# A hybrid decoder layer on one core: the order of requests, splits, evacuations and constants in the first stage is changed

## The chip, the core and the metric

The program runs on one NeuronCore of a Trainium2 chip, in one launch. TensorE multiplies, VectorE and ScalarE split and evacuate, GpSimd does side work and issues DMAs on a queue of its own, and SyncE issues the large loads. The metric is the device time of a run in microseconds. Three runs of the kernel before took 1409.1, 1410.75 and 1412.94 us, with a median of 1410.75. The trace is of a further, profiled execution.

## The reference

One layer over 1024 tokens of width 1024, in float32:

```python
h = rms_norm(x, norm_mix)
z = h @ w_in                       # u, v of a gated MLP; q, k, values of attention
u, v = gelu(zu), gelu(zv)          # spatial gating, 4 groups, chunks of 128 tokens
a_out = u * (tril(W_s) @ layer_norm(v) + b)
lam = exp(sum(lq1*lk1)) - exp(sum(lq2*lk2)) + lambda_init
o = diff_attention(q, k, vv, lam)  # 4 heads, 2 causal softmax maps each, ALiBi
o = rms_norm(o, diff_subln) * (1 - lambda_init)
x = x + concat(a_out, o) @ w_out
x = x + memory_attention(rms_norm(x, norm_xq), rms_norm(mem, norm_mem), w_q, w_kv, w_o)
x = x + hierarchical_moe(rms_norm(x, norm_ffn), ...)   # 4 groups of 8 experts, top 2
return rms_norm(x, norm_final)
```

`mem` has 256 tokens; its keys and values are `rms_norm(mem) @ w_kv`, 2048 columns in all.

## The kernel before

Matmuls that need float32 accuracy are made of three. Each operand is split into a rounded part and a rest: ScalarE writes the first (`whi`, `hTh`, `mh`), VectorE subtracts and writes the second (`wlo`, `hTl`, `ml`), and `mm3` adds three products. Lines 141 to 143 are these three matmuls; lines 285 and 286 split a weight tile, 150 and 151 a scaled activation.

All weights come as tiles of 128 x 1024 (512 KB) in the order of one list, `plan`. `pump` requests tiles on SyncE's queue up to `ahead["load"]` tiles beyond the one in use and splits up to `ahead["split"]` beyond it; `take` hands out the next one. SBUF is 45 slots of one tile (`unit`), which a request may have to wait for. Smaller things lie in 7 half slots (`half`): the copies of memory's keys and values (`km`), and the scaled q or k (`pr`). PSUM has four single banks (`ps1`) and two double ones (`ps2`). The copies that the kernel makes by DMA (`kmd`, `vmd`, the halves of k) go out on GpSimd's queue.

The work is in three parts, each a run of generators in `merge`, which advances a clock of its own by the costs and delays that they yield and so interleaves them. In the first part the engines' order is exactly the order in which the code is recorded. In the second and third a scheduler orders TensorE, VectorE and ScalarE by a timeline of its own, and what it finds ready early it places among the last instructions of the first part; SyncE and GpSimd keep the recorded order. Then the experts follow, again in recorded order. Because the scheduler works on, a change in the first part also moves instructions in the next.

The first part, where the change is:

- `x_prep` (line 428) loads x transposed, eight tiles of 128 x 1024, and for each k splits it to `hTh`, `hTl`. The square of tile k-1 (in place, line 434, after its split has read it) stands behind that; even squares are added up by VectorE, odd ones by GpSimd (line 436). Behind the eighth tile the sums meet (452), eight small matmuls and a reciprocal root give the norm `xcol`, and transposes spread it to `rx` (464, 466). The splits don't wait for the norm: it is multiplied in when a product is evacuated.
- `first_qk` (line 505) multiplies each x tile, as it comes, with the weights of q and k of head 0: 12 matmuls of 512 columns per tile, into the two double banks `pd`. When `rx` is there, `evacs` (line 553) evacuates them: multiply by `rx` (472), round (566 or 577), subtract (567 or 579); the halves of k are also copied to the other 64 partitions by DMA (578, 580), for q's and k's rounded and rest parts are stacked.
- `mem_kv` (line 314) makes memory's keys and values: 16 weight tiles, each 24 matmuls of 256 columns (`pmk`), copied (329) and stored (330). Before the first it loads and splits memory itself, two tiles (`memt`, `mh`, `ml`). In tiles 9 and 10 memory is squared and reduced (336, 337); the norm `mcol` follows at the end (343), and `mem_row` (345) transposes it to a row (354).
- The constants come when `rx` is done, in the order in which the generator is reached: `sgu_consts` (735; line 737 requests the SGU weights, 738 masks them on GpSimd), `sgu_bias` (746; a matmul of the masked weights with ones, 749, and four additions, 751), `attn_consts` (536, lambda), `small_consts` (1005).

The scores of the second part (`scores`, lines 632 and 633) multiply q tiles with `ka` and `la`, then `kb` and `lb`, into the same two double banks, and add a bias (635) that GpSimd makes (612, 614).

Of the kernel before, what the change touches and what calls it, by code (L numbers as in the profile page):

```python
# [13 lines left out]
OP = mybir.AluOpType  # L14
# [48 lines left out]
R2 = 0.009  # L63
AT = 2.6
LIM = "q2:sc0 v1:sc0 q3:sc1"
A0 = 1
A1 = 5
A2 = 3
A3 = 2
RC = ('P', 3, 1)  # L70
PS = 4
# [43 lines left out]
def tile_layer(tc, a, out):  # L115
# [12 lines left out]
    def unit(name, shape, dt=F32):  # L128
        return up.tile(shape, dt, name=name, tag="u", bufs=NU)
# [182 lines left out]
    mrow = {}  # L312

    def mem_kv(i):
        if i == 0:
            for q in range(2):
                load_mem(q)
                split_mem(q)
                yield 0.0, 0.0
        for c in range(4 * i, 4 * i + 4):  # L320
            wh, wl = take()
            p = ps1("pmk")
            for k in range(KT):
                q, r = divmod(k, 4)
                mm3(p[:, :256], wh[:, k], wl[:, k], mhl[q][0][:, r], mhl[q][1][:, r], k == 0, k == KT - 1)
                if k == 3:
                    yield 1.3, 0.0
            km = half("km", (128, 256))
            nc.scalar.copy(km, p[:, :256])
            nc.gpsimd.dma_start((kmd, vmd)[c // 8][:, c % 8, :], km)  # L330
            yield 1.3, 0.0
            if c in (9, 10):
                q = c - 9
                if q == 0:
                    macc[0] = half("macc", (128, 2, 256))
                nc.scalar.activation(memt[q], memt[q], AF.Square)
                red(macc[0][:, q], memt[q].rearrange("p k t -> p t k"), axis=AX.X, op=OP.add)
        if i < 3:
            return
        pm = ps1("pm")  # L340
        for t in range(2):
            for q in range(2):
                mm(pm[:, 2 * t:2 * t + 2], macc[0][:, q, t * 128:(t + 1) * 128], ones[:, 0:2], start=(q == 0),
                   stop=(q == 1))
        rsq(mcol, pm[:, 0:4:2], D, 1e-6, "m")
        done.add("mcol")
# [163 lines left out]
    def first_qk(hd):  # L510

        w = [take() for _ in range(2)]
        p = [ps2() for _ in range(2)]
        for k in range(KT):
            for x in until(("x", k)):
                yield x
            for i in range(2):
                for h in range(2):
                    hs = slice(h * H, (h + 1) * H)
                    mm3(p[i][:, hs], w[i][0][:, k], w[i][1][:, k], hTh[k][:, hs], hTl[k][:, hs], k == 0, k == KT - 1)  # L520
            yield 2.56, 0.0
        done.add("first")
        ahead["load"], ahead["split"] = A1, A2
        for x in until("rx"):
            yield x
        qk[hd] = []
        for evac, q in zip(evacs(hd), p):
            for h in range(2):
                evac(h, q[:, h * H:(h + 1) * H])
                yield 0.0, 0.0  # L530
        done.add(("qk", hd))


# [4 lines left out]
    def attn_consts():  # L538
        for i, n in enumerate(("lambda_q1", "lambda_k1", "lambda_q2", "lambda_k2")):
            row(lam4[:, i], a[n], 64)  # L540
        nc.gpsimd.dma_start(subg, a["diff_subln"])
        for i in range(2):
            nc.vector.scalar_tensor_tensor(lam4[:, 2 * i], lam4[:, 2 * i], 1.0, lam4[:, 2 * i + 1], op0=OP.mult,
                                           op1=OP.mult, accum_out=lam[:, i:i + 1])
        nc.scalar.activation(lam[:, 2:4], lam[:, 0:2], AF.Exp)
        nc.vector.scalar_tensor_tensor(lam[:, 0:1], lam[:, 2:3], 0.8 - 0.6 * math.exp(-0.0), lam[:, 3:4],
                                       op0=OP.add, op1=OP.subtract)

# [4 lines left out]
    def evacs(hd):  # L553


        r0, r1 = slice(0, 64), slice(64, 128)

        def evac_q(h, p):
            hs = slice(h * H, (h + 1) * H)
            if h == 0:  # L560
                qk[hd] += [unit(n, [128, S], F32R) for n in ("qa", "qb")]
            qa, qb = qk[hd]
            q = scaled(h, p)
            sc = 0.125 / slopes[hd]
            for t, r, o in ((qa, r0, r1), (qb, r1, r0)):
                nc.scalar.activation(t[r, hs], q[r], AF.Copy, scale=sc)
                nc.vector.scalar_tensor_tensor(t[o, hs], q[r], sc, t[r, hs].bitcast(F32), op0=OP.mult,
                                               op1=OP.subtract)

        def evac_k(h, p):  # L570
            hs = slice(h * H, (h + 1) * H)
            if h == 0:
                qk[hd] += [unit(n, [128, S], F32R) for n in ("ka", "kb", "la", "lb")]
            ka, kb, la, lb = qk[hd][2:]
            k = scaled(h, p)
            for t, l, r, o in ((ka, la, r0, r1), (kb, lb, r1, r0)):
                nc.scalar.copy(t[r, hs], k[r])
                KQ(nc).dma_start(t[o, hs], t[r, hs])
                nc.vector.tensor_sub(l[r, hs], k[r], t[r, hs].bitcast(F32))
                KQ(nc).dma_start(l[o, hs], l[r, hs])  # L580

        return evac_q, evac_k

    def proj_qk(hd):
        qk[hd] = []
        for evac in evacs(hd):
            for x in proj_t(evac):
                yield x
        done.add(("qk", hd))
# [20 lines left out]
    def scores():  # L610
# [5 lines left out]
        for hd in range(4):  # L616
            for x in until(("qk", hd)):
                yield x
            qa, qb, ka, kb, la, lb = qk.pop(hd)
            for i in range(8):  # L620
                if 8 * hd + i - 2 * ndone[0] >= NA:
                    yield 0.0, lambda: 8 * hd + i - 2 * ndone[0] < NA
# [112 lines left out]
    def sgu_consts():  # L735
        w = unit("sgw", [128, 2, 4, 128])
        nc.gpsimd.dma_start(w[:, 0], a["sgu_wT"].rearrange("g s t -> s g t"))
        nc.gpsimd.affine_select(w[:, 0], w[:, 0], pattern=[[0, 4], [1, 128]], compare_op=OP.is_ge, fill=0.0, base=0,
                                channel_multiplier=-1)
        lg = sm.tile([128, 8], F32, name="lngb")  # L740
        nc.gpsimd.dma_start(lg[:, 0:4], a["sgu_ln_g"])
        nc.gpsimd.dma_start(lg[:, 4:8], a["sgu_ln_b"])
        row(w[:, 1].rearrange("p g t -> p (g t)"), a["sgu_b"], 512)
        sg["w"], sg["g"] = w, lg

    def sgu_bias():
        w, lg = sg["w"], sg["g"]
# [576 lines left out]
    nc.sync.dma_start(gmix, a["norm_mix"])  # L1324
    ahead["load"], ahead["split"] = 1, 1
    pump()
    ahead["load"] = A0
    gm[0] = col("norm_mem")
    gxq = col("norm_xq")
    gffn = col("norm_ffn")  # L1330
# [2 lines left out]
    def side(text):  # L1333

        g = [sgu_gate(i) for i in range(2) if "s%d" % i in text]
        if "k3" in text:
            g.append(mem_row())
        return g

    merge.run(x_prep(), *side(SEQ1), run_items(SEQ1.split()[0]),  # L1340
              seq(until("first"), run_items(SEQ1[3:])), seq(until("rx"), now(sgu_consts), now(sgu_bias), now(attn_consts),
                                                            now(small_consts)))
    man.__exit__(None, None, None)
    ahead["load"], ahead["split"] = AL, A3
    man = tc.manual_schedule(engines=ORDS[1])
# [348 lines left out]
```

## Time and profile before

| | |
|---|---|
| median of three runs | 1410.75 us (1409.1 to 1412.94) |
| profiled execution | 1409.82 us, its span 1408.1 us |
| TensorE, VectorE, ScalarE, GpSimd busy | 94%, 71%, 59%, 19% of the span |
| first stage (to the last memory matmul) | about 0 to 94 us |
| bytes moved | 322.39 MB, 229 GB/s on average |

The profile is one execution. "PE" is TensorE, "DVE" VectorE, "ACT" ScalarE, "POOL" GpSimd, "SPq" SyncE's queue. In a timeline a row is: start, duration, engine, line, operation, out<-in, shapes, count, and in brackets the idle time of the engine before it and what ended it. [...] Matmuls overlap, so a matmul's row is longer than its share of the time. The duration of a row with a count above 1 is that of all of them together.

### The profile page before, as it was taken

The page shows a single profiled execution, that of the slowest core. Times are in us where ns is not written, and L with a number is a line of the kernel's source. Part 1 is how long each engine was busy: PE and PEld are TensorE (multiplying, and loading weights), DVE is VectorE, ACT ScalarE, POOL GpSimd, SP SyncE. Part 2 cuts the span into 40 slices and gives each one's busy share as a digit, 9 for nine tenths or more (in the row PEclk, how much of TensorE's full clock was granted, in tenths as well). Part 3 has the DMA queues.
Part 4 walks back from the last instruction along what each step waited for, and adds up shares of the span by engine and source line. Part 5 has one row for each costly group of instructions (what it writes and reads, how often), then busy time and mean ns, then how long its engine had stood idle before and what let it go on. Part 6 is the DMA issues. An engine that isn't in the chain of part 4 may idle for free. (4 is left out here: it accounts for less than half of the span.)

```text
span 1408.1 us, 20553 instructions
## 1 busy us (share of the span) xinstructions
PE 1325.6 (94%) x7424; PEld 1148.1 (82%) x7424; DVE 1001.1 (71%) x1594; ACT 833.9 (59%) x1138; POOL 262.0 (19%) x287
## 2 busy tenths in 40 slices
PE   7889999999989999999999799999999999999981
PEld 5889898889887888999888587888777888888861
DVE  6646785676856444333454798999979999999975
ACT  7534463455454453333232588888868888888863
POOL 3231110301102231112112111111111111111012
PEclk9989999999999999999999799999999999999996
DMA  8550211212265666012689899999999699999985
GB/s 307 156 139 2 61 46 60 76 39 61 76 220 198 210 216 210 1 61 81 224 319 324 275 327 377 367 358 358 354 373 331 224 369 381 371 356 363 375 288 225
DMA packets 103225, 322.39 MB, mean 229 GB/s; under 512 B 15747, under 2 KB 23971, under 8 KB 103120
## 3 DMA queue, kind: packets, MB, share of 16 engines
q1 hardware_dynamic: 76896, 272.14, 52.8%
q0 software_dynamic: 17776, 40.51, 10.3%
q10 hardware_dynamic: 8448, 8.39, 1.8%
q8 instruction: 59, 0.97, 0.3%
q14 instruction: 46, 0.38, 0.1%
HBM read 287.10 MB, written 46.66 MB: 237 GB/s over the span
## 5 line engine op out<-in xcount | busy, mean ns | idle before, releaser
L286 DVE TENSOR_TENSOR wlo<-raw,whi 128x1024 fp32r<-128x1024 f32 (+1 forms) x469 | 556.2, 1225 | 84.5 <-ACT whi L285 72.7
L285 ACT CAST whi<-raw 128x1024 fp32r<-128x1024 f32 (+1 forms) x469 | 471.6, 1049 | 62.9 <-DVE wlo L286 11.2
L141 PE MATMUL pgu<-whi,xth 128*128 128x512 f32 x512 | 198.7, 397 | 4.5 <-ACT whi L285 3.4
L142 PE MATMUL pgu<-wlo,xth 128*128 128x512 f32 x512 | 200.9, 392 | 1.1 <-DVE wlo L286 1.1
L143 PE MATMUL pgu<-whi,xtl 128*128 128x512 f32 x512 | 200.4, 391 | 0.5 <-DVE xtl L147 0.5
L1424 POOL DMA_INDIRECT x2d<-y,idx x31 | 50.3, 1621 | 450.0 <-ACT y L1423 412.4
L141 PEld LDWEIGHTS pgu<-whi,xth 128*128 128x128 f32 x512 | 96.8, 189 | 26.1 <-ACT whi L285 5.3
L142 PEld LDWEIGHTS pgu<-wlo,xth 128*128 128x128 f32 x512 | 96.8, 189 | 22.6 <-DVE wlo L286 2.5
L143 PEld LDWEIGHTS pgu<-whi,xtl 128*128 128x128 f32 x512 | 96.7, 189 | 21.1 <-DVE xtl L147 1.2
L141 PE MATMUL py<-whi,ht 128*128 128x512 f32 x256 | 103.0, 402 | 4.4 <-ACT whi L285 2.2
L142 PE MATMUL py<-wlo,ht 128*128 128x512 f32 x256 | 104.4, 408 | 2.2 <-DVE wlo L286 2.1
L143 PE MATMUL py<-whi,ht 128*128 128x512 f32 x256 | 101.1, 395 | 0.0
L639 ACT ACTIVATE p<-p,stt 128x128 f32<-128x128 f32 (+7 forms) x64 | 49.6, 776 | 49.7 <-DVE stt L638 40.8
L142 PE MATMUL pp<-wlo,hTh 128*128 128x256 f32 x256 | 73.1, 285 | 1.5 <-DVE wlo L286 1.5
L141 PE MATMUL pp<-whi,hTh 128*128 128x256 f32 x256 | 73.4, 287 | 0.2 <-ACT whi L285 0.2
L141 PE MATMUL pp<-whi,h2h 128*128 128x256 f32 x256 | 73.1, 285 | 0.0
L143 PE MATMUL pp<-whi,hTl 128*128 128x256 f32 x256 | 72.8, 285 | 0.0
L142 PE MATMUL pp<-wlo,h2h 128*128 128x256 f32 x256 | 72.5, 283 | 0.0
L143 PE MATMUL pp<-whi,h2l 128*128 128x256 f32 x256 | 72.5, 283 | 0.0
L141 PE MATMUL pp<-hTh,whi 128*128 128x512 f32 x160 | 64.3, 402 | 0.4 <-ACT ot L691 0.4
L142 PE MATMUL pp<-hTl,whi 128*128 128x512 f32 x160 | 63.6, 398 | 0.0
L143 PE MATMUL pp<-hTh,wlo 128*128 128x512 f32 x160 | 63.5, 397 | 0.0
(365 smaller groups left out, 2956.9 us busy)
## 6 DMA issues: line engine op xcount, KB each, us to landing
raw<-in_w_gate SPq DMA_DIRECT2D x128, 512.0 KB
raw<-in_w_up SPq DMA_DIRECT2D x128, 512.0 KB
raw<-in_w_down SPq DMA_DIRECT2D x128, 512.0 KB
raw<-in_w_in SPq DMA_DIRECT2D x19, 512.0 KB
raw<-in_w_kv_mem SPq DMA_DIRECT2D x16, 512.0 KB
raw<-vwd SPq DMA_DIRECT2D x16, 512.0 KB
raw<-in_w_q_memT SPq DMA_DIRECT2D x8, 512.0 KB
raw<-in_w_out SPq DMA_DIRECT2D x8, 512.0 KB
```

The costliest lines, as they stand in the source:

```text
L141: mm(o, sh, mh, start=start, stop=False)
L142: mm(o, sh, ml, start=False, stop=False)
L143: mm(o, sl, mh, start=False, stop=stop)
L285: nc.scalar.copy(hi[:, c], raw[:, c])
L286: ahead.get("lo", nc.vector).tensor_tensor(lo[:, c], raw[:, c], hi[:, c].bitcast(F32), op=OP.subtract)
L639: nc.scalar.activation(pe[:, :nk], pe[:, :nk], AF.Exp, bias=stt[:, 2 + m:3 + m], scale=slopes[hd], accum_out=stt[:, 4 + m:5 + m])
L1424: nc.gpsimd.indirect_dma_start(out=x2d[:, :], out_offset=bass.IndirectOffsetOnAxis(ap=idx[:, e:e + 1], axis=0), in_=y, in_offset=None, bou ...
```

## The change

The parts of the diff:

- `A0` is 0 in place of 1: the first memory weight tile is no longer requested ahead of x1. When x3 has come (`k == 3`), five memory weight tiles and both memory tiles are requested. With k = 5, 6, 7 the number of tiles to split grows by one each, and behind x6 and x7 a memory tile is split (`split_mem`). `A2`, the splits ahead from the end of x on (3), is thereby replaced.
- The four evacuations of head 0 are k's two halves, then q's, each with a delay of `EV` = 3.5 in the generator's clock behind it; before, q's and k's followed each other. Therefore `qk` becomes a dictionary.
- `first_consts` requests the SGU and attention constants when the splits of x are recorded (`hT`); the mask, the small constants, lambda and the SGU bias follow after `rx`, spread by delays.
- `mem_row` runs in the second part.

```diff
-A0 = 1
+A0 = 0
+EV = 3.5
 A1 = 5
-A2 = 3
...
     def mem_kv(i):
-        if i == 0:
-            for q in range(2):
-                load_mem(q)
-                split_mem(q)
-                yield 0.0, 0.0
         for c in range(4 * i, 4 * i + 4):
...  # first_qk, in the loop over k, behind the matmuls
+            if k == 3:
+                ahead["load"], ahead["split"] = A1, 0
+                pump()
+                load_mem(0)
+                load_mem(1)
+            if k > 4:
+                if k > 5:
+                    split_mem(k - 6)
+                ahead["split"] += 1
+                pump()
             yield 2.56, 0.0
         done.add("first")
-        ahead["load"], ahead["split"] = A1, A2
...
-        qk[hd] = []
-        for evac, q in zip(evacs(hd), p):
+        qk[hd] = {}
+        for i in (1, 0):
             for h in range(2):
-                evac(h, q[:, h * H:(h + 1) * H])
-                yield 0.0, 0.0
+                evacs(hd)[i](h, p[i][:, h * H:(h + 1) * H])
+                yield 0.0, EV
...  # attn_consts keeps the requests; its arithmetic goes to attn_lam, the mask to sgu_mask
+    def attn_lam():
         for i in range(2):
             nc.vector.scalar_tensor_tensor(lam4[:, 2 * i], ...)
+        yield 0.0, 4.0
         nc.scalar.activation(lam[:, 2:4], lam[:, 0:2], AF.Exp)
+        yield 0.0, 4.0
         nc.vector.scalar_tensor_tensor(lam[:, 0:1], ...)
...
-    ahead["load"] = A0
+    ahead["load"], ahead["split"] = A0, 0
...
-        if "k3" in text:
+        if text == SEQ2:
             g.append(mem_row())
...
+    def first_consts():
+        for x in until("hT"):
+            yield x
+        sgu_consts()
+        attn_consts()
+        for x in until("rx"):
+            yield x
+        yield 0.0, 2.0
+        sgu_mask()
+        small_consts()
+        for x in attn_lam():
+            yield x
+        yield 0.0, 6.0
+        sgu_bias()
+        yield 1.0, 0.0
-    merge.run(x_prep(), *side(SEQ1), run_items(SEQ1.split()[0]),
-              seq(until("first"), run_items(SEQ1[3:])), seq(until("rx"), now(sgu_consts), now(sgu_bias), now(attn_consts),
-                                                            now(small_consts)))
+    merge.run(x_prep(), *side(SEQ1), run_items(SEQ1.split()[0]), first_consts(),
+              seq(until("first"), run_items(SEQ1[3:])))
```

What stands where on the engines, first the requests on SyncE from x0 on. `xt` are the x tiles, `raw` the weight tiles, `memt` memory. Before:

```order
L443 DMA xt<-in_xT 128x512 x2
L276 DMA raw<-in_w_in 128x1024
L276 DMA raw<-in_w_kv_mem 128x1024
L443 DMA xt<-in_xT 128x1024 x7
L303 DMA memt<-in_memT 128x1024 x2
L276 DMA raw<-in_w_kv_mem 128x1024 x15
```

and now:

```order
L438 DMA xt<-in_xT 128x512 x2
L276 DMA raw<-in_w_in 128x1024
L438 DMA xt<-in_xT 128x1024 x3
L276 DMA raw<-in_w_kv_mem 128x1024 x5
L303 DMA memt<-in_memT 128x1024 x2
L438 DMA xt<-in_xT 128x1024 x4
L276 DMA raw<-in_w_kv_mem 128x1024 x11
```

Five tiles of memory weights and the two of memory moved from behind x7 to between x3 and x4; the one memory weight tile that stood ahead of x1 is among them.

The second place is VectorE from the split of x1 on (the lines of x: 151 writes `hTl`, 436 and now 431 adds squares, 452 and now 447 joins the sums). Before:

```order
L151 SCALAR_TENSOR_TENSOR hTl<-xt,c_mix,hTh 128x1024 x3
L436 TENSOR_TENSOR xt<-xt 128x1024
L151 SCALAR_TENSOR_TENSOR hTl<-xt,c_mix,hTh 128x1024 x2
L436 TENSOR_TENSOR xt<-xt 128x1024
L151 SCALAR_TENSOR_TENSOR hTl<-xt,c_mix,hTh 128x1024 x2
L436 TENSOR_TENSOR xt<-xt 128x1024
L452 TENSOR_TENSOR xt<-xt 128x1024
L151 SCALAR_TENSOR_TENSOR ml<-memt,c_norm_mem,mh 128x256 x8
L286 TENSOR_TENSOR wlo<-raw,whi 128x1024 x6
```

and now:

```order
L151 SCALAR_TENSOR_TENSOR hTl<-xt,c_mix,hTh 128x1024 x3
L431 TENSOR_TENSOR xt<-xt 128x1024
L151 SCALAR_TENSOR_TENSOR hTl<-xt,c_mix,hTh 128x1024 x2
L431 TENSOR_TENSOR xt<-xt 128x1024
L286 TENSOR_TENSOR wlo<-raw,whi 128x1024
L151 SCALAR_TENSOR_TENSOR hTl<-xt,c_mix,hTh 128x1024
L151 SCALAR_TENSOR_TENSOR ml<-memt,c_norm_mem,mh 128x256 x4
L286 TENSOR_TENSOR wlo<-raw,whi 128x1024
L151 SCALAR_TENSOR_TENSOR hTl<-xt,c_mix,hTh 128x1024
L431 TENSOR_TENSOR xt<-xt 128x1024
L151 SCALAR_TENSOR_TENSOR ml<-memt,c_norm_mem,mh 128x256 x4
L286 TENSOR_TENSOR wlo<-raw,whi 128x1024
```

Two weight splits and the first half of memory's now stand between the splits of x5 and x7, and the second half of memory's ahead of the joining of the sums.

The third place is TensorE near the first scores and the SGU bias. `pmk` are the memory matmuls, `ps_s` the scores; before, the first score stands behind 216 of the 384 memory matmuls:

```order
L143 MATMUL pmk<-mh,wlo 128x256
L632 MATMUL ps_s<-ka,qa 128x128
L633 MATMUL ps_s<-la,qa 128x128
L632 MATMUL ps_s<-kb,qb 128x128
L141 MATMUL pmk<-mh,whi 128x256
L142 MATMUL pmk<-ml,whi 128x256
```

Now its `ka` and `la` matmuls stand behind 290 of them. The SGU matmul, which stood behind all of them and the norm of memory, and the second pair of scores stand behind 312:

```order
L143 MATMUL pmk<-mh,wlo 128x256
L763 MATMUL ps<-sgw,ones 128x512
L643 MATMUL ps_s<-kb,qb 128x128
L644 MATMUL ps_s<-lb,qb 128x128
L141 MATMUL pmk<-mh,whi 128x256
```

On GpSimd, which the SGU matmul waits for, the end of the first part before was (`vmd` are stores of memory's values):

```order
L330 DMA vmd<-km 128x256 x8
L737 DMA sgw<-in_sgu_wT 128x4x128
L738 AFFINE_SELECT sgw<-sgw 128x512
L741 DMA lngb<-in_sgu_ln_g 128x4
L742 DMA lngb<-in_sgu_ln_b 128x4
```

The request for `sgw` now stands directly behind the third addition of squares, ahead of all stores, and the mask behind six stores and the first copies of k:

```order
L325 DMA kmd<-km 128x256 x5
L588 DMA ka<-ka 64x512
L590 DMA la<-la 64x512
L588 DMA kb<-kb 64x512
L590 DMA lb<-lb 64x512
L325 DMA kmd<-km 128x256
L757 AFFINE_SELECT sgw<-sgw 128x512
L1020 MEMSET cb 128x128
```

## Rows read from the trace of the kernel before

**Rows 1.** The page's first part, busy time of each engine:
```profile
PE 1325.6 (94%) x7424; PEld 1148.1 (82%) x7424; DVE 1001.1 (71%) x1594; ACT 833.9 (59%) x1138; POOL 262.0 (19%) x287
```

**Rows 2.** Windows behind the first stage: stretch us, length, busy us (x) by engine, PEclk, DMA:
```profile
110.00:433.00 323.00, 314.27 (x2042) 284.96 (x2040) 226.59 (x628) 162.84 (x302) 54.12 (x73) 0.99 0.25 77
433.00:1408.00 975.00, 922.01 (x4802) 781.53 (x4802) 707.64 (x875) 613.94 (x756) 175.14 (x159) 0.97 0.79 283
```

**Rows 3.** Waits from 0 to 104 us: who <- whom, us in total, times, longest:
```profile
PE ps L749 <- POOL sgw L738: 5.0, 1, 5.0
...
PE ps_s L632 <- DMA kb<-kb: 3.8, 1, 3.8
...
PE pmk L142 <- DVE ml L151: 1.4, 1, 1.4
...
PE ps_s L632 <- DMA ka<-ka: 0.9, 1, 0.9
...
PE ps_s L633 <- DMA la<-la: 0.8, 1, 0.8
```

**Rows 4.** Windows around the two long waits, columns as in Rows 2:
```profile
64.15:70.34 6.19, 0.63 (x3) 0.40 (x3) 4.78 (x6) 5.63 (x10) 4.03 (x8) 0.93 1.17 215
70.34:76.33 5.99, 5.99 (x27) 5.97 (x28) 1.93 (x2) 0.67 (x1) 1.09 (x2) 0.50 0.69 209
76.33:82.00 5.67, 5.67 (x50) 5.67 (x49) 4.21 (x3) 4.54 (x6) 1.08 (x2) 1.00 0.65 195
94.45:99.49 5.04, 0.01 (x1) 0.00 (x1) 1.80 (x11) 0.00 (x0) 1.93 (x4) 0.73 0.26 80
99.49:103.63 4.14, 4.14 (x13) 3.00 (x14) 0.00 (x0) 0.00 (x0) 4.14 (x8) 0.50 0.51 71
```

**Rows 5.** Timeline of SyncE: start us, us, instruction, count:
```profile
10.14 0.33 SPq L303 DMA_DIRECT2D memt<-in_memT  x1
...
17.83 0.33 SPq L276 DMA_DIRECT2D raw<-in_w_kv_mem  x1
```

**Rows 6.** Timeline of ScalarE, first stage; in brackets idle time before and its releaser:
```profile
10.15 1.04 ACT L285 CAST whi<-raw 128x1024 fp32r<-128x1024 f32 x1 [0.20 <-DMA raw<-in_w_kv_mem]
11.44 1.15 ACT L150 ACTIVATE hTh<-xt,c_mix 128x1024 fp32r<-128x1024 f32 x1 [0.24 <-DMA xt<-in_xT]
...
18.46 1.04 ACT L434 ACTIVATE xt<-xt 128x1024 f32<-128x1024 f32 x1
...
30.25 3.29 ACT L150 ACTIVATE mh<-memt,c_norm_mem 128x256 fp32r<-128x256 f32 x8
...
41.44 0.38 ACT L329 COPY km<-pmk 128x256 f32<-128x256 f32 x1 [2.19 <-PE pmk L143]
```

**Rows 7.** Timeline of VectorE, the same stretch:
```profile
9.99 2.46 DVE L286 TENSOR_TENSOR wlo<-raw,whi 128x1024 fp32r<-128x1024 f32 x2 [1.23 <-ACT whi L285]
12.62 1.28 DVE L151 SCALAR_TENSOR_TENSOR hTl<-xt,c_mix,hTh 128x1024 fp32r<-128x1024 f32 x1 [0.17 <-ACT hTh L150]
...
20.58 2.99 DVE L151 SCALAR_TENSOR_TENSOR hTl<-xt,c_mix,hTh 128x1024 fp32r<-128x1024 f32 x1 [0.36 <-ACT hTh L150]
...
29.17 1.21 DVE L436 TENSOR_TENSOR xt<-xt 128x1024 f32<-128x1024 f32 x1
...
34.07 3.25 DVE L151 SCALAR_TENSOR_TENSOR ml<-memt,c_norm_mem,mh 128x256 fp32r<-128x256 f32 x8
```

**Rows 8.** Timeline of GpSimd, its additions of squares:
```profile
19.59 2.90 POOL L436 TENSOR_TENSOR xt<-xt 128x1024 f32<-128x1024 f32 x1 [16.20 <-ACT xt L434]
...
30.49 2.40 POOL L436 TENSOR_TENSOR xt<-xt 128x1024 f32<-128x1024 f32 x1 [2.32 <-ACT xt L434]
```

**Rows 9.** Timeline of TensorE: x1's second matmul, x4's first, the first memory matmul:
```profile
13.96 0.50 PE L142 MATMUL pd<-hTl,whi 128*128 128x512 f32 x1 [0.83 <-DVE hTl L151]
...
22.02 0.39 PE L141 MATMUL pd<-hTh,whi 128*128 128x512 f32 x1
...
32.91 0.28 PE L141 MATMUL pmk<-mh,whi 128*128 128x256 f32 x1
```

More of the change, by code (lines that the diff above doesn't have):

```diff
@@ L560, in evac_q @@
             if h == 0:
-                qk[hd] += [unit(n, [128, S], F32R) for n in ("qa", "qb")]
-            qa, qb = qk[hd]
+                qk[hd].update((n, unit(n, [128, S], F32R)) for n in ("qa", "qb"))
+            qa, qb = qk[hd]["qa"], qk[hd]["qb"]
             q = scaled(h, p)
@@ L572, in evac_k @@
             if h == 0:
-                qk[hd] += [unit(n, [128, S], F32R) for n in ("ka", "kb", "la", "lb")]
-            ka, kb, la, lb = qk[hd][2:]
+                qk[hd].update((n, unit(n, [128, S], F32R)) for n in ("ka", "kb", "la", "lb"))
+            ka, kb, la, lb = [qk[hd][n] for n in ("ka", "kb", "la", "lb")]
             k = scaled(h, p)
@@ L584, in proj_qk @@
     def proj_qk(hd):
-        qk[hd] = []
+        qk[hd] = {}
         for evac in evacs(hd):
@@ L618, in scores @@
                 yield x
-            qa, qb, ka, kb, la, lb = qk.pop(hd)
+            qs = qk.pop(hd)
+            qa, qb, ka, kb, la, lb = [qs[n] for n in ("qa", "qb", "ka", "kb", "la", "lb")]
             for i in range(8):
@@ L737, in sgu_consts @@
         nc.gpsimd.dma_start(w[:, 0], a["sgu_wT"].rearrange("g s t -> s g t"))
-        nc.gpsimd.affine_select(w[:, 0], w[:, 0], pattern=[[0, 4], [1, 128]], compare_op=OP.is_ge, fill=0.0, base=0,
-                                channel_multiplier=-1)
         lg = sm.tile([128, 8], F32, name="lngb")
@@ L744, in sgu_consts, with sgu_mask @@
         sg["w"], sg["g"] = w, lg
+    def sgu_mask():
+        w = sg["w"]
+        nc.gpsimd.affine_select(w[:, 0], w[:, 0], pattern=[[0, 4], [1, 128]], compare_op=OP.is_ge, fill=0.0, base=0,
+                                channel_multiplier=-1)
     def sgu_bias():
```

## The prediction

> **What bounds the kernel now.** I read the page's first part, then busy time by stretch, then the waits of the first stage, then the instructions of that stage engine by engine. TensorE is busy for 94% of the span [rows 1]. After the first stage it has little to give: 314.27 of 323 us between 110 and 433 us and 922.01 of 975 us behind that [rows 2]. In those stretches a matmul mostly waits for another matmul, so time won or lost by TensorE before 110 us is handed on about one for one.
>
> The first stage has the visible waits [rows 3]. The score matmuls wait for the copied halves of k (0.9, 0.8 and 3.8 us), one matmul waits for the SGU weights that GpSimd masks (5.0 us), the first memory matmuls wait for `ml` (1.4 us). The stretches show the price in full [rows 4]. From 64.15 to 70.34 TensorE works 0.63 of 6.19 us, 5.56 lost. Then it runs at a granted clock of 0.50 (1.2 GHz) to 76.33: 27 matmuls in 5.99 us, where at full clock 50 took 5.67, 0.113 each. 27 would have taken 3.06, so 2.93 are lost. From 94.45 to 99.49 the wait for `sgw` loses 5.03, and the clock stays at 0.50 until 103.63: half of 4.14, 2.07. Together 5.56 + 2.93 + 5.03 + 2.07 = **15.6 us**.
>
> **What removes them.** Nothing is computed more or less; all is order. (1) The SGU weights are requested behind the last sum of squares and masked in the middle of the stage, so `sgw` is ready more than 10 us before its matmul: 5.03 + 2.07 go. That matmul's own time stays. Its successor, the norm of memory, no longer stands on TensorE's path, because its two transposes went into the next stage among value matmuls. (2) k is evacuated first, and the first score stands after 290 of the 384 memory matmuls in place of 216, the second pair after 312. The score's operands come out of evacuations one to three, of which the last begins when 8 of 16 tiles (192 matmuls) are done. 98 matmuls at 0.113 are 11 us for 3 us of work: 5.56 + 2.93 go.
>
> I checked what could be late next. In the back half VectorE has one `wlo` (2.46 / 2 = 1.23, [rows 7]) per tile of 24 matmuls (2.7 us at 0.113), plus four evacuations of three operations and two reductions over memory. That nearly fills it, but `wlo` now stands between the evacuations, three tiles ahead. Stepping through the order I find one wait of about 0.4 us, at the 15th tile, behind the second reduction. I take **0.4**, with 0 to 4 as bounds (4 would be two operations of 1.2 to 2 us in front of a `wlo` without the lead). The nine constants cost GpSimd about 5 us of issuing at a time when it has nothing else; the exponential of lambda is one tiny ScalarE operation. Both 0; the cover is the three-tile lead.
>
> **What it adds: x comes late.** This is the large cost. The order of requests puts five tiles of memory weights and two of memory before x4. x4 was the 8th tile of 512 KB and is now the 14th. SyncE's requests wake when the tile eight requests earlier lands: the 4th tile at 10.14, the 10th at 17.83 [rows 5], 1.28 each, and ScalarE takes the 4th up at 10.15 [rows 6]. The 14th lands at 17.83 + 4 x 1.28 = 22.95, x5 to x7 at 24.2, 25.5 and 26.8.
>
> TensorE first gains: a weight tile is no longer split ahead of x1, which also lands a tile earlier (10.14, `hTh` to 11.30, `hTl` to 12.6). Its second matmul starts at 12.6 in place of 13.96 [rows 9]. x4 began at 22.02 and could begin at 20.6. But `hTh` of x4 runs 22.96 to 24.1 (1.15, [rows 6]), `hTl` to 25.4 (1.28, [rows 7]): the second matmul of x4 starts at 25.4, not 20.9, **4.6 late**.
>
> From there VectorE sets the pace, because the weight and memory splits now stand between x5 and x7, and because of GpSimd's sums. A VectorE operation that begins while GpSimd adds is held: `hTl` at 20.58 took 2.99 in place of 1.28 and ended at 23.57, 1.08 after GpSimd's addition (19.59 + 2.90 = 22.49) [rows 7, 8]. Alone, that addition takes 2.40 [rows 8]. Step by step:
> - The square of x3 stands behind `hTh` of x4 and ends at 25.05 (1.04 each, [rows 6]). GpSimd adds until 27.8; `hTl` of x5 ends at 28.9.
> - VectorE's own addition (1.21) ends at 30.0, GpSimd's next begins at 30.1 behind the square of x5. Whichever goes first, `wlo` and `hTl` of x6 with that addition between take until 34.7.
> - Four `ml` (3.25 / 2 = 1.6), one `wlo` (1.23) and `hTl` of x7 (1.28): 38.8.
>
> TensorE needs 12 matmuls per x tile, 2.72 us ((32.91 - 22.02) / 4, [rows 9]). It starts the second matmul of x5 at 28.9, of x6 at 34.7, of x7 at 38.8, and is through at 41.3; before that was 32.91. The second half of memory is then held by GpSimd's last addition (40.0 to 42.4): its four `ml` end at 43.9, so the first memory tile ends near 44.35 and the second, with the copy that follows it, near 47.4. Before, the copy behind the second tile began at 41.44 [rows 6], already with the 1.4 us wait for `ml` inside. So the stage is **6.0 us** late here.
>
> The bounds of this term: if only the landing of x4 counted and VectorE caught up, 4.6 - 1.4 (the lead won at x1) - 1.4 (the `ml` wait) = 1.8. If the clock falls as well and stays down, an x tile takes 2 x 2.72 = 5.44 and a memory tile 24 x 5.99 / 27 = 5.3 [rows 4]: x7 ends at 25.2 + 4 x 5.44 = 47.0, the first memory tile at 52.3, 8.0 behind the 44.35. So 1.8 to 14. I take 6.0, and 0.7 for the clock, because the rows show it back 6 and 4 us after matmuls resumed [rows 4], which here falls into the wait for x6.
>
> **Sum.** -15.6 + 6.0 + 0.4 + 0.7 = -8.5 us. The later stages keep TensorE's total work, their order differs only up to about 430 us, and transposes and their uses stand equally far apart there; I take 0, bounds -3 to +3. The profiled execution took 1409.82 us for a span of 1408.1, so 1401.3 on its scale. The median of the runs is 1410.75, 0.9 above; on that scale **1402.3 us**.
>
> **Rivals.**
> - *x costs next to nothing* (chance 0.10). The late tiles are caught up, the term is 1.8 and the clock holds: -15.6 + 1.8 + 0.4 = -13.4, 1397.4 us. For it: ScalarE has a gap at most x tiles. Against: VectorE's held operations, which the trace shows in this very stretch.
> - *New waits replace the old* (0.16). VectorE is nearly full in the back half; each reduction or evacuation that slips puts a `wlo` behind TensorE. The 4 us bound and one more fall of the clock (2.9): -8.5 + 3.6 + 2.9 = -2.0, 1408.8 us, no change that can be told.
> - *It doesn't do what it says* (0.04). If the mask's place in GpSimd's queue, behind the copies of k, made `sgw` late again, 5.03 + 2.07 stay: -1.4, 1409.4 us. Against: GpSimd is idle for most of the stage.
> - *The array starves at half clock, slower* (0.10). The mechanism: from 20.6 on each x tile waits, the clock falls, and at 1.2 GHz TensorE itself takes 5.4 us per x tile, and goes on so through the memory tiles. The first memory tile would end 8.0 later, as worked out above; each further one at half costs 24 x (0.222 - 0.113) = 2.6 more. It decides from the third further tile on: -15.6 + 6.0 + 0.4 + 8.0 + 3 x 2.6 = +6.6, 1417.4 us. For it: both long waits of the first stage brought the clock down [rows 4], and the first new wait is about as long. Against: the matmuls stand back to back once x4 is in, and in both rows the clock came back under that.
>
> [...]
>
> **How the numbers follow.** The forecast's own case, -4 to -12.5, has 0.60. A measurement of this kernel can tell 0.3%, about 4.2 us, from no change. Faster by more: 0.60 + 0.10 = 0.70. Within: 0.16 + 0.04 = 0.20. Slower by more: 0.10. The range goes from the first rival (with 1 us more) to the median before: 1396 to 1411; what is left out is most of the slower case and a gain beyond 14 us.
>
> **What would show it.** Right: `hTh` of x4 starts near 23 us and waits for a DMA; TensorE is idle for some 4 to 5 us before it; `hTl` of x5 or a `wlo` near 30 us takes 2.5 to 3.5 us; the copy behind the second memory tile starts near 47 us; no wait of scores for k and none for `sgw`; the value matmuls run at full clock from about 93 to 95 us, where full clock came at 103.63 before. Wrong: `hTl` of x7 done by 34 us (then x costs little), or a clock of 0.5 past 45 us, or `pmk` matmuls waiting for `wlo` by more than 2 us in total behind 60 us.

## The result and the profile after

The changed kernel takes 1400.03 us (median of 4 runs, 1399.09 to 1402.13), the kernel before 1410.92 us (median of 4 runs beside it). The ratio is 0.9927, 95% interval [0.9915, 0.9938]: 0.7% faster. The profiled execution took 1400.26 us with a span of 1398.6, where before had 1409.82 and 1408.1, so 9.5 us of span are to be found. TensorE's busy time, which answers to [rows 1], fell by only 3.5 us; the rest is idle time that is gone:

```profile
PE 1322.1 (95%) x7424; PEld 1144.4 (82%) x7424; DVE 1005.8 (72%) x1594; ACT 834.4 (60%) x1138; POOL 261.1 (19%) x287
```

The waits of TensorE from 0 to 104 us (columns as in [rows 3]) have no `sgw`, no `kb`, `ka` or `la` and no `ml` any more. In their place stand waits for x. Of the 10.2 us in the first row, 7.7 are the start of the kernel, and 2.5 are the wait for x4:

```profile
PE pd L141 <- ACT hTh L150: 10.2, 2, 7.7
...
PE pd L142 <- DVE hTl L151: 2.3, 3, 0.9
```

The stretches of the first stage (columns as in [rows 2]) show the same in TensorE's busy time, the first column behind the length, and in PEclk, the granted clock as a share of the full one:

```profile
16.66:24.30 7.64, 5.60 (x25) 4.32 (x23) 1.71 (x2) 0.91 (x2) 0.00 (x0) 1.00 1.03 409
24.30:31.13 6.83, 5.81 (x13) 4.24 (x14) 5.65 (x4) 6.83 (x9) 2.90 (x2) 0.50 0.46 168
31.13:41.61 10.48, 8.74 (x37) 6.52 (x36) 10.48 (x11) 8.66 (x13) 4.24 (x2) 1.00 0.18 60
62.00:92.33 30.33, 30.11 (x244) 29.23 (x243) 25.25 (x33) 19.88 (x31) 11.27 (x26) 1.00 0.76 218
93.14:99.11 5.97, 5.97 (x53) 5.97 (x52) 5.38 (x18) 1.20 (x3) 2.61 (x3) 1.00 0.06 22
```

The second row is the half clock behind the wait for x4: 24.30 to 31.13, 13 matmuls. The fourth answers to the two long waits of [rows 4]: from 62 us to the last memory matmul TensorE now works 30.11 of 30.33 us. The last shows the first value matmuls at full clock, 53 in 5.97 us. In the trace of before, matmuls of 512 columns begin 0.43 us apart at a PEclk of 0.50 (251.15 to 253.29 us) and 0.23 apart at 1.00 (254.46 to 255.82), matmuls of 256 columns 0.213 apart at 0.50 (72.08 to 75.92). 256 columns in 0.213 us are 1.2 per ns; the prediction's 1.2 GHz stands for this rate.

Where it came from, by the start of the same matmul in both traces. The first memory matmul starts at 41.61 instead of 32.91 [rows 9]. From the 49th memory matmul on, behind the waits for `ml` and `wlo` of before, the lateness is 6.12 us (47.36 against 41.24). At the 289th it is already a lead of 3.18 (78.80 against 81.98), because the waits for the scores are gone and the scores themselves now stand behind it. At the 49th value matmul, where both run at full clock, the lead is 9.24 (99.11 against 108.35). In the rest it rises to 12.3 us and falls back to 9.5 at the end. Two stretches of before and one of the changed kernel show most of it:

```profile
250.40:253.81 3.41, 3.41 (x10) 2.63 (x9) 2.25 (x9) 0.00 (x0) 0.00 (x0) 0.50 0.01 2
769.23:789.71 20.48, 10.19 (x62) 9.04 (x61) 15.60 (x59) 4.55 (x8) 4.78 (x4) 0.50 0.88 288
```

```profile
754.75:782.06 27.31, 16.46 (x83) 14.53 (x83) 18.16 (x62) 8.20 (x13) 5.71 (x4) 0.50 0.73 233
```

Before fell to half clock at 250.40; the changed kernel did not fall there. In the routing of the experts (from about 750 us) it was the changed kernel that stayed at half clock longer, 27.31 us against 20.48.

### The profile page after: what moved, and what is told of

Its sections match the earlier page's. It is cut to its first block, busy times and chain, and to the rows that moved or that the text cites. A ratio compares the mean times of both kernels' runs of the same rounds, so it can differ in the third digit from the quotient of the medians.

```text
span 1398.6 us, 20561 instructions
## 1 busy us (share of the span) xinstructions
PE 1322.1 (95%) x7424; PEld 1144.4 (82%) x7424; DVE 1005.8 (72%) x1594; ACT 834.4 (60%) x1138; POOL 261.1 (19%) x287
```

## The experiments

Each was compared with the kernel before on the same chip; differences between two of these kernels, below, are between medians, some of them from different chips. The last column is the start of the 49th value matmul (`pp`, the products that follow memory's) in its profile: the first stage alone, without what the clock does behind it.

| kernel | median us | ratio to before, 95% interval | 49th value matmul, us |
|---|---|---|---|
| before | 1410.92 | 1 | 108.35 |
| the change | 1400.03 | 0.9927 [0.9915, 0.9938] | 99.11 |
| only x late | 1414.51 | 1.0026 [1.0016, 1.0035] | 113.44 |
| constants and norm rows back | 1404.99 | 0.9963 [0.9949, 0.9976] | 105.74 |
| norm rows back | 1406.40 | 0.9977 [0.9968, 0.9987] | 105.76 |
| constants back | 1406.72 | 0.9969 [0.9957, 0.9981] | 105.34 |
| evacuations back | 1409.62 | 0.9991 [0.9980, 1.0003] | 108.02 |
| x first | 1395.34 | 0.9899 [0.9885, 0.9914] | 93.30 |
| x between | 1396.21 | 0.9898 [0.9882, 0.9914] | 93.20 |
| x between, sums on VectorE | 1393.79 | 0.9886 [0.9872, 0.9900] | 92.38 |
| x between, splits last | 1393.31 | 0.9873 [0.9859, 0.9888] | 91.82 |
| all three | 1394.35 | 0.9897 [0.9882, 0.9912] | 90.98 |
| sums on VectorE | 1400.11 | 0.9923 [0.9910, 0.9935] | 96.88 |
| x first, sums on VectorE | 1399.60 | 0.9923 [0.9909, 0.9936] | 94.96 |

**Only x late.** Of the change the move of the requests and splits alone (the three other edits are undone, as each is below).

```diff
-        for i in (1, 0):
+        for i in (0, 1):
...
-                yield 0.0, EV
+                yield 0.0, 0.0
...
+              seq(until("rx"), now(sgu_consts), now(sgu_mask), now(sgu_bias), now(attn_consts), ...)
...
-        if text == SEQ2:
+        if text == SEQ1:
             g.append(mem_row())
```

> Of the change only the move of the requests and splits is kept (tiles 4 to 7 of x asked for as the 11th to 14th tile instead of the 5th to 8th, memory's weights split while x comes in); the constants, the order of the evacuations and the place of memory's norm rows are those of before. Theory (the late x costs about 6 us in the first 42 us, and the three other edits save 15.6 us of waits and half clock between 64 and 104 us): the kernel is slower than before by 6.0 us, 1416 to 1418 us, first memory matmul near 41.6 us instead of 32.9, with both old waits (scores on kb about 4 us, sgw about 5 us) back. Rival (the late requests themselves free the queues or the engines in the back half and so bring part of the gain): 1411 us or less, and the waits of 64 to 104 us are shorter than 8 us in sum.

Slower than before by 0.26%, 3.7 us on 1410.4 (4.1 by the medians), against the 6.0 expected. Both old waits are back: 0.9 + 0.6 + 3.2 us for `ka`, `la` and `kb`, 5.0 for `sgw` (columns as in [rows 3]).

```profile
PE ps L763 <- POOL sgw L757: 5.0, 1, 5.0
PE ps_s L643 <- DMA kb<-kb: 3.2, 1, 3.2
```

In the profiled execution the span is 5.1 us longer than before's, and so is the first stage (113.44 against 108.35). The sign is right, the time is under the expected 1416 to 1418, and the rival is out: the early requests don't free the back half. The size is below 6.0, partly because the score waits are 0.8 us shorter than the 5.56 of before.

**Evacuations back.** Of the edits above the first two hunks, so that the four evacuations follow each other in a burst again, q's first:

```diff
-        for i in (1, 0):
+        for i in (0, 1):
...
-                yield 0.0, EV
+                yield 0.0, 0.0
```

> The changed kernel with the evacuations of the first head in one burst, queries first, as before has them; constants and requests as changed. Theory (the burst alone made the score waits, 5.56 us, and the half clock behind them, 2.93 us): 1408.5 us, 8.5 us above the changed kernel, with TensorE waiting for kb, ka or for the memory halves near 62 to 75 us. Rival (the burst costs only where the constants' requests stand in GpSimd's queue at the same time, and these are now out of the way): under 1403 us, no wait over 1 us there.

1409.62, that is 9.6 above the changed kernel, and 8.91 at the 49th value matmul, for 8.49 = 5.56 + 2.93 expected. The scores wait although the constants are out of GpSimd's way, so undoing this edit alone brings the wait back. TensorE's row (columns as in [rows 9]), then the copies of `kb` in GpSimd's queue (count, KB, median us from request to landing), first of this kernel, then of the changed one:

```profile
77.33 0.45 PE L643 MATMUL ps_s<-kb,qb 128*128 128x128 f32 x1 [5.15 <-DVE wlo L286]
```

```profile
kb<-kb POOLq DMA_DIRECT2D x2, 128.0 KB, 7.0
```

```profile
kb<-kb POOLq DMA_DIRECT2D x2, 128.0 KB, 4.1
```

The profile names `wlo`, but this matmul reads `kb` and `qb`. The first copy of `kb` was requested at 69.52 and landed 7.7 us later, at 77.19, just before the matmul. This is how a name is to be checked: by what the waiting instruction reads.

The slow copy is not all of it. With the evacuations back, the scheduler also puts the first score behind 216 memory matmuls again, as in before, in place of 290. Here the first copy of `kb` is requested 1.6 us before the first score (69.52 and 71.16), in the changed kernel 14.4 us before it (64.67 and 79.04); there a copy of 7.7 us would have been in time too. The order of the halves, the delay `EV` and the place of the scores came back together, so the run doesn't say what each is worth.

**Constants and norm rows back.** Both edits undone, then each alone.

```diff
-    merge.run(x_prep(), *side(SEQ1), run_items(SEQ1.split()[0]), first_consts(),
-              seq(until("first"), run_items(SEQ1[3:])))
+    merge.run(x_prep(), *side(SEQ1), run_items(SEQ1.split()[0]),
+              seq(until("first"), run_items(SEQ1[3:])),
+              seq(until("rx"), now(sgu_consts), now(sgu_mask), now(sgu_bias), now(attn_consts), ...))
...
-        if text == SEQ2:
+        if text == SEQ1:
             g.append(mem_row())
```

> The changed kernel with the constants asked for where before asks for them (after the memory halves have been stored) and memory's norm rows where they were. Theory (the sgw wait of 5.03 us and its 2.07 us of half clock are a term of their own): 1407.1 us, 7.1 us above the changed kernel, with one wait of TensorE for sgw of about 5 us near 93 us and none for ka, kb or the masks. Rival (the two waits shared one delay, so that with one gone the other is hidden or doubled): under 1403 us, or over 1411 us.

1404.99 is 5.0 above the changed kernel, less than the 7.1 expected and more than the rival's bound; in the first stage it is 6.63. The wait for `sgw` is there:

```profile
PE ps L763 <- POOL sgw L757: 4.6, 1, 4.6
```

But the two edits were undone together, so it doesn't say which of them counts.

**Norm rows back.** The second hunk alone:

```diff
-        if text == SEQ2:
+        if text == SEQ1:
             g.append(mem_row())
```

> The changed kernel with only memory's norm rows back in the first stage (two transposes behind the matmuls of pm, a copy on ScalarE). Theory (two small transposes and a copy whose input is ready cost nothing that can be measured): 1400 us, within 1.5 us of the changed kernel. Rival (TensorE now waits for VectorE's chain of eight small operations that makes mcol, which the wait for sgw covered in before): 1402 to 1404 us, with a wait of 2 to 3 us behind pm near 93 us.

The theory fell. 1406.40 is 6.4 us above the changed kernel, more than the rival asked for, and the first stage is as late as with both edits undone (105.76 against 105.74). The two transposes wait for `mcol`, though the SGU weights are ready. TensorE's row, and VectorE's chain that makes `mcol` from `pm`, the sums of memory's squares (its first four rows and the last):

```profile
96.97 0.44 PE L349 MATMUL pm<-ident,mcol 128*128 128x128 f32 x1 [4.12 <-DVE mcol L165]
```

```profile
92.89 0.16 DVE L157 TENSOR_SCALAR w_m<-pm 128x2 f32<-128x2 f32 x1 [1.08 <-PE pm L338]
93.09 1.26 DVE L158 TENSOR_SCALAR w_m<-w_m 128x2 int32<-128x2 int32 x1
94.38 0.16 DVE L161 SCALAR_TENSOR_TENSOR w_m<-w_m 128x2 f32<-128x2 f32 x1
94.58 0.88 DVE L162 TENSOR_TENSOR w_m<-w_m 128x2 f32<-128x2 f32 x1
...
96.67 0.16 DVE L165 SCALAR_TENSOR_TENSOR mcol<-w_m 128x2 f32<-128x2 f32 x1
```

Eleven operations on two columns take from 92.89 to 96.83, and two of them take 1.26 and 0.88 us. The wait is 4.12, and the clock is at half from 95.39 to 102.22.

**Constants back.** The first hunk alone.

> The changed kernel with only the constants back where before asks for them; memory's norm rows stay one stage later. The run before it showed that the norm rows alone, put back, cost 6.4 us by a wait of 4.1 us for mcol. Theory (two waits stood behind each other in the same 5 us of before, one for sgw and one for mcol, so either edit alone saves nothing): 1405 to 1407 us, with a wait of 4.5 to 5 us for sgw behind pm and none for mcol. Rival (the wait for mcol is the one that counts, and with the rows gone the sgw matmul is late by little): 1400 to 1402 us.

1406.72 is 6.7 us above the changed kernel, as the theory had it; the first stage stands at 105.34. TensorE waits for `sgw`, not for `mcol`:

```profile
96.47 1.22 PE L763 MATMUL ps<-sgw,ones 128*128 128x512 f32 x1 [4.54 <-POOL sgw L757]
```

So in the kernel before, two waits lay on top of each other in the same 5 us. Either alone costs the whole 6 to 7 us, and only both edits together win them.

**x first.** The move of the requests and splits undone, the three other edits kept:

```diff
-            if k == 3:
-                ahead["load"], ahead["split"] = A1, 0
-                pump()
-                load_mem(0)
-                load_mem(1)
...
     def mem_kv(i):
+        if i == 0:
+            for q in range(2):
+                load_mem(q)
+                split_mem(q)
```

> The changed kernel with only the move of the requests and splits undone: x's tiles 4 to 7 are asked for first and memory's weights are split behind them, as before has it; constants, staggered evacuations and memory's norm rows as changed. Theory (the late x is a pure loss, and the three other edits do not need it): 1395 us, 15.6 us below before and about 5 us below the changed kernel, first memory matmul near 33 us with its wait of about 1.4 us for ml, no wait for kb or sgw. Rival (the early requests are what makes the back half run without waits): 1398 to 1400 us, with new waits for wlo or raw tiles between 35 and 64 us.

1395.34, as expected, 4.7 us below the changed kernel (5.81 in the first stage), with the wait for `ml` of before:

```profile
PE pmk L143 <- DVE ml L152: 1.4, 1, 1.4
```

The late x is a pure loss; nothing in the back half needed it.

**x between.** The same requests, with one of memory's between each two of x's:

```diff
-            if k == 3:
-                ahead["load"], ahead["split"] = A1, 0
-                pump()
-                load_mem(0)
-                load_mem(1)
+            if 2 < k:
+                ahead["load"] += 1
+                pump()
+            if k in (4, 5):
+                load_mem(k - 4)
```

> The changed kernel with the same requests in another order: a tile of memory's weights or of memory between each two of x's tiles 4 to 7, instead of all seven ahead of them. Theory A (x's tile 4 comes late because seven requests stand ahead of it, and that alone idles TensorE by 3.0 us and puts it at half clock for 6.83 us, worth 3.4): 1394.5 to 1396 us, 4 to 5.5 us faster than the changed kernel, hTh of tile 4 begins at about 19 us, and the granted clock stays full through 24 to 31 us. Theory B (VectorE's chain, held behind GpSimd's additions at tiles 5, 6 and 7, sets the pace and x's lateness only hides it): 1398 to 1399 us, 1 to 2 us faster, with TensorE still waiting for hTl before x6 and x7.

1396.21, 3.8 us below the changed kernel. `hTh` of x4 starts at 18.74, and the clock stays full through 24 to 31 us: theory A, 0.2 above its range. What is left is theory B's sign. One wait, with a half clock of 3.41 us behind it:

```profile
31.52 0.55 PE L142 MATMUL pd<-hTl,whi 128*128 128x512 f32 x1 [2.50 <-DVE hTl L151]
```

```profile
24.11 1.27 DVE L151 SCALAR_TENSOR_TENSOR hTl<-xt,c_mix,hTh 128x1024 fp32r<-128x1024 f32 x1
25.31 3.82 DVE L151 SCALAR_TENSOR_TENSOR ml<-memt,c_norm_mem,mh 128x256 fp32r<-128x256 f32 x4
29.05 1.21 DVE L286 TENSOR_TENSOR wlo<-raw,whi 128x1024 fp32r<-128x1024 f32 x1
30.19 1.27 DVE L151 SCALAR_TENSOR_TENSOR hTl<-xt,c_mix,hTh 128x1024 fp32r<-128x1024 f32 x1
```

VectorE's rows say why. `hTl` of x6 (the last row) stands behind four `ml`, and these took 3.82 us in place of 1.67; one of them, which ran beside an addition of GpSimd's, took 2.63 in place of 0.47.

**x between, splits last.**

```diff
-                if k > 5:
-                    split_mem(k - 6)
+                if k == 7:
+                    split_mem(0)
+                    split_mem(1)
```

> Requests of x and memory interleaved as in the run before it, and both memory tiles split behind x's tile 7 instead of one ahead of tile 6 and one ahead of tile 7. Theory (the last wait of the x phase, 2.5 us for hTl of tile 6, is there because four ml and a GpSimd hold stand ahead of hTl on VectorE): 1393.5 to 1394.5 us, 2 to 3 us below the interleaved kernel, no wait over 0.5 us before tile 6, no half clock at 32 us. Rival (the wait only moves to ml before the first memory matmul, as in before with 1.42 us): 1395 to 1396 us.

1393.31, 2.9 us below the interleaved kernel (1.38 in the first stage), and no half clock at 32 us. Waits of 0.84 us for `hTl` of x6 and 0.95 for `ml` stay, the first more than the 0.5 expected. This is the fastest of all by its median: 1.3% below before, and below the changed kernel too.

**x between, sums on VectorE.**

```diff
-                (nc.vector, nc.gpsimd)[k % 2].tensor_tensor(
+                (nc.vector, nc.vector)[k % 2].tensor_tensor(
```

> Requests interleaved as before, and all sums of squares on VectorE, none on GpSimd. Theory (VectorE operations that run beside a GpSimd addition are stretched, hTl to 1.99 us and one ml to 2.63 us instead of 1.28 and 0.47): the stretched ones fall back, the 2.5 us wait for hTl of tile 6 shrinks to about 1.5 us, 1395 to 1396 us, 0.3 to 1.2 us below the interleaved kernel. Rival (four additions of 1.21 us more on VectorE cost as much as the holds): 1396 to 1397 us, the same or slower.

1393.79, 2.4 us below the interleaved kernel, more than expected; but the intervals of the two ratios overlap, and in the first stage it is 0.82, within the 0.3 to 1.2 expected. The four `ml` are back at 1.67 us, `hTl` of x6 begins as its `hTh` allows, and TensorE's waits at x6 are 0.62 and 0.82, the 1.5 expected:

```profile
25.31 1.28 DVE L151 SCALAR_TENSOR_TENSOR hTl<-xt,c_mix,hTh 128x1024 fp32r<-128x1024 f32 x1 [0.54 <-ACT hTh L150]
...
27.65 1.67 DVE L151 SCALAR_TENSOR_TENSOR ml<-memt,c_norm_mem,mh 128x256 fp32r<-128x256 f32 x4
29.23 1.23 DVE L286 TENSOR_TENSOR wlo<-raw,whi 128x1024 fp32r<-128x1024 f32 x1
30.62 1.28 DVE L151 SCALAR_TENSOR_TENSOR hTl<-xt,c_mix,hTh 128x1024 fp32r<-128x1024 f32 x1 [0.16 <-ACT hTh L150]
```

**All three.**

> Three edits on the changed kernel together: requests of x and memory interleaved, all sums of squares on VectorE, both memory tiles split behind x's tile 7. Theory (one wait, the 2.5 us for hTl of tile 6 with its half clock, is what the second and the third edit each removed, so they don't add up): 1392.5 to 1394 us, as each of them alone, with a wait for ml of about 1 us left before the first memory matmuls. Rival (they add up, 2.4 + 2.9 us below the interleaved kernel): 1391 us.

1394.35, a little above the range of the theory, and not to be told apart from either edit alone. Its first stage is the earliest of all, 90.98. From 17 to 84 us TensorE hardly waits. Far behind that its trace has a stretch at half clock that "splits last" doesn't have:

```profile
17.00:84.00 67.00, 66.75 (x485) 62.69 (x485) 54.15 (x73) 43.54 (x64) 19.02 (x40) 1.00 0.74 236
232.78:236.19 3.41, 3.41 (x10) 2.64 (x9) 2.43 (x10) 0.00 (x0) 0.00 (x0) 0.50 0.01 2
```

This doesn't explain the median: the execution that has this stretch took 1391.80 us, the fastest of the four, and the profiled one of "splits last" 1394.36. Why the median is not lower stays open.

**Sums on VectorE**, on the changed kernel alone.

> The changed kernel with all sums of squares on VectorE and none on GpSimd. Theory A (behind the late x, VectorE's chain with holds of 1.35 us at hTl5 and 2.2 us at hTl6 sets the pace of tiles 6 and 7): 1398 to 1399 us, 1 to 2 us below the changed kernel, no hTl or ml of VectorE over 1.7 us between 14 and 44 us. Theory B (the lateness of tile 4 alone sets it): within 0.7 us of the changed kernel.

By the time, theory B: 1400.11 against 1400.03. By the trace, theory A: TensorE waits 1.6 us for `hTl` in place of 2.3, and the first stage ends 2.23 us earlier (96.88 against 99.11). In the profiled execution the gain was given back behind it (its span is 1399.1 against 1398.6), in part here, where the changed kernel kept the full clock:

```profile
237.99:241.40 3.41, 3.41 (x9) 2.66 (x9) 3.03 (x13) 0.52 (x1) 0.00 (x0) 0.50 0.01 2
```

**x first, sums on VectorE.**

> x's tiles asked for first, as before has it, memory's weights split behind them, and all sums of squares on VectorE; the rest as changed. Theory (with the requests of x out of the way, GpSimd's holds are the cause of the 1.4 us wait for ml before the first memory matmuls): the wait falls under 0.7 us and the kernel to 1393.5 to 1394.5 us, about 1 us below the kernel with x first alone. Rival (four additions more on VectorE are as long as the holds): 1395 to 1396 us with the wait unchanged or longer.

Neither: 1399.60, 4.3 us slower than x first alone (1.66 in the first stage). The wait for `ml` is gone, but x came late by another way. With no addition in its queue, GpSimd had nothing ahead of the constants and requested them at once. GpSimd and ScalarE of this kernel (the request of the SGU weights; `hTh` of x1 and x2):

```profile
3.37 0.77 POOL L745 DMA_DIRECT2D sgw<-in_sgu_wT  x1
```

```profile
13.33 1.15 ACT L151 ACTIVATE hTh<-xt,c_mix 128x1024 fp32r<-128x1024 f32 x1 [1.12 <-DMA xt<-in_xT]
...
16.93 1.15 ACT L151 ACTIVATE hTh<-xt,c_mix 128x1024 fp32r<-128x1024 f32 x1 [1.51 <-DMA xt<-in_xT]
```

and the same rows of "x first":

```profile
33.16 0.79 POOL L745 DMA_DIRECT2D sgw<-in_sgu_wT  x1
```

```profile
11.79 1.15 ACT L151 ACTIVATE hTh<-xt,c_mix 128x1024 fp32r<-128x1024 f32 x1 [0.24 <-DMA xt<-in_xT]
...
13.79 1.13 ACT L151 ACTIVATE hTh<-xt,c_mix 128x1024 fp32r<-128x1024 f32 x1
```

With nine transfers of constants among x's tiles, x1 was 1.5 us late and x2 3.1, and TensorE ran from 14.64 to 21.47 at half clock. What had kept the constants behind x was the additions ahead of them on the queue. In the other kernels without these additions the request also moved forward, but only to between 17.76 and 18.94 us: there it waited some 15 us for one of VectorE's additions (`xt`, line 431).

## Why the prediction was right

**x comes late, +6.0.** Measured 6.12 in the trace; x first wins back 5.81 in the first stage and 4.7 in the medians. The steps hold one after the other: `hTh` of x4 at 23.59 (forecast 22.96), `hTl` of x7 done at 38.92 (38.8), x through at 41.61 (41.3), the second memory copy at 47.56 (47.4). ScalarE's, VectorE's and GpSimd's rows, which answer to [rows 6 to 8], and TensorE's:

```profile
23.59 1.15 ACT L150 ACTIVATE hTh<-xt,c_mix 128x1024 fp32r<-128x1024 f32 x1 [6.73 <-DMA xt<-in_xT]
...
47.56 0.37 ACT L324 COPY km<-pmk 128x256 f32<-128x256 f32 x1 [1.56 <-PE pmk L143]
```

```profile
24.77 1.28 DVE L151 SCALAR_TENSOR_TENSOR hTl<-xt,c_mix,hTh 128x1024 fp32r<-128x1024 f32 x1 [6.40 <-ACT hTh L150]
26.76 2.62 DVE L151 SCALAR_TENSOR_TENSOR hTl<-xt,c_mix,hTh 128x1024 fp32r<-128x1024 f32 x1 [0.70 <-ACT hTh L150]
...
31.57 3.44 DVE L151 SCALAR_TENSOR_TENSOR hTl<-xt,c_mix,hTh 128x1024 fp32r<-128x1024 f32 x1
...
37.65 1.27 DVE L151 SCALAR_TENSOR_TENSOR hTl<-xt,c_mix,hTh 128x1024 fp32r<-128x1024 f32 x1
```

```profile
25.77 2.53 POOL L431 TENSOR_TENSOR xt<-xt 128x1024 f32<-128x1024 f32 x1 [22.38 <-ACT xt L429]
30.76 3.17 POOL L431 TENSOR_TENSOR xt<-xt 128x1024 f32<-128x1024 f32 x1 [2.46 <-ACT xt L429]
...
42.65 0.79 POOL L748 DMA_DIRECT2D sgw<-in_sgu_wT  x1
...
66.28 0.66 POOL L757 TENSOR_SCALAR_AFFINE_SELECT sgw<-sgw 128x512 f32<-128x512 f32 x1
```

```profile
24.79 0.79 PE L141 MATMUL pd<-hTh,whi 128*128 128x512 f32 x1 [2.53 <-ACT hTh L150]
...
41.61 0.28 PE L141 MATMUL pmk<-mh,whi 128*128 128x256 f32 x1
...
93.14 0.36 PE L141 MATMUL pp<-whi,hTh 128*128 128x256 f32 x1
```

The held operations are the forecast's: `hTl` of x5 takes 2.62 us and ends at 29.38, that of x6 takes 3.44 and ends at 35.01, each 1.08 us behind the end of GpSimd's addition (28.30 and 33.93), as in [rows 7, 8]. The `hTl` of x4 and x7, which begin while GpSimd doesn't add, take 1.28 and 1.27. In "x between, sums on VectorE", where GpSimd adds nothing, the four `hTl` between 18 and 32 us took 1.28 or 1.29. What in an addition holds them isn't shown.

One step was too good. x1's lead of 1.4 us, by which x4 "could begin at 20.6", did not appear: x2's matmuls began at 16.66 against 16.59 before, since x1's weights were split 0.6 us later (9.50 against 8.91) and full clock came at 14.06 instead of 11.47. It changed nothing, because x4's landing and VectorE's chain behind it set the end; it only made the idle time ahead of x4 3.06 us (2.53 + 0.53) in place of 4 to 5.

**The clock, +0.7, and the `wlo` wait, +0.4.** The clock fell for 6.83 us, and its cost lies inside the 6.12, hidden in the wait for x6, as the prediction said of most of it. "Only x late" shows it: its clock did not fall there, and from x2's first to the first memory matmul it took 25.05 us against 24.95. The `wlo` wait was 0.2. The two terms were 1.1 in the sum and close to nothing in the trace.

**Score waits and their clock, -8.49.** The burst put back costs 8.91 in the first stage and 9.6 in the medians. The step holds, with less room than forecast: the third evacuation began at 72.54, behind 236 memory matmuls and not 192, and its last result was there at 75.39, 3.65 us before the first score, where 11 - 3 = 8 us were forecast. VectorE's rows of it, its first and its last operation:

```profile
72.54 0.68 DVE L467 TENSOR_TENSOR pr<-pd,rx 128x512 f32<-128x512 f32 x1
...
74.70 0.69 DVE L577 SCALAR_TENSOR_TENSOR qb<-pr,qb 64x512 fp32r<-64x512 f32 x1
```

What order, delay and the place of the scores are worth one by one stays open (above).

**`sgw` and its clock, -7.10.** Put back, 6.63 in the first stage and 5.0 in the medians. The sum holds, its grounds only half. The prediction put the term to the constants, and gave the move of memory's norm rows one sentence and no price. The runs show the saving needs both: either edit alone would have left it at 0 to 0.4 us (first stage 105.76 and 105.34, with neither 105.74). With the norm rows left in place, the same working would have forecast -8.5 and missed by some 6 us.

**The later stages, 0 (-3 to +3).** -12.3 near 454 us and -9.5 at the end, for -9.24 behind the first stage: inside the bounds at the end. That the two nearly cancel is luck: half clocks of before at 250 and of the changed kernel at 755 us went opposite ways.

Together: 6.12 + 0.2 - 8.91 - 6.63 - 0.3 = -9.5, the difference of the spans. 1401.3 on the profiled execution's scale was forecast and 1400.26 came (1402.3 and 1400.03 by the medians, 2.3 apart, since the profiled execution of before lay 0.9 below the median used and that of the changed kernel 0.2 above its own). On the profiled scale the miss of 1.0 is about the 0.9 by which the two small terms were too high; that the misses of the others (+0.1, -0.4, +0.5 and -0.3) cancel is luck. Of the rivals, "new waits replace the old" and "the array starves" are out: no wait of TensorE over 0.2 us between 41.61 and 157 us, and the clock is full from 31.13, 6.3 us behind x4's first matmul, to 403. "It doesn't do what it says" is out, for `sgw` was masked at 66.94, 15 us before its matmul (81.90). "x costs next to nothing" is out by x first.

## What to carry to other kernels

Behind a wait that was removed here stood the next one (4.54 us for `sgw`, 4.12 for `mcol`): look at what the following instruction on that engine waits for, and price the pair, since either edit alone won at most 0.4 us of the first stage and both won 6.63. Transfers asked for early are to be priced at what they are put in front of: ahead of x4 they cost 5.81 us of the first stage, and interleaved with x, the same requests cost nothing that can be told beside x first (93.20 and 93.30). GpSimd's additions also held back the requests behind them in its queue (`sgw` requested at 33.16 us with them, at 3.37 without); before an instruction moves to another engine, look at what it was holding.

## What was not expected of the hardware

The clock behind the same short wait is not the same from trace to trace. Some 145 us behind the first value matmul TensorE waits 0.57 or 0.58 us, in each of the 14 traces. In 7 of them (before, "norm rows back", and all from "x first" on in the table but "x between" and "splits last") the granted clock then was at half for 3.41 or 6.83 us, in 7 it stayed full. Behind the wait for x4 (2.53 to 3.28 us in the seven kernels with x late) it was at half for 6.83, 3.41 or 0 us, and the longest stretch stood behind the shortest waits. Which trace gets which is open. There is one trace of each kernel, so it need not hang on the kernel: over the 22 runs of before beside the first experiments the mean granted clock went from 0.966 (a run of 1413.82 us) to 0.973 (1407.55). Such a stretch took part of the 2.23 us in the trace of "sums on VectorE". Differences of 1 to 2 us between these kernels' medians, and 1393 to 1395 us above all, can't be ordered by these runs.
